# Overflow branch ahead of the slots' table, a second embedding quarter behind it, and token rows stored even columns first

## The chip, the cores and the metric

The kernel runs on one core of a Trainium2 chip. The metric is the device time of one execution in microseconds. Three runs of the kernel before gave 1337.99, 1342.89 and 1343.95, median 1342.89. Engines are named as the profile names them: PE is TensorE, PEld its weight load, DVE is VectorE, ACT is ScalarE, POOL is GpSimd, SP is SyncE.

## What is computed

Two layers of a streaming encoder over 512 tokens of 1024 columns. The first half of a layer (three kinds of attention, an output projection, a layer norm) gives the rows h. The change sits in the second half, a mixture of 16 experts, two for each token, and a gated embedding of four column quarters:

```python
scores = jax.nn.sigmoid((h @ router_w).astype(jnp.float32))
...
best_group = jnp.argmax(group_score, axis=-1)
...
_, idx = lax.top_k(masked, TOP_K)
...
for e in range(N_EXPERTS):
    hid = jax.nn.silu(h @ w_gate[e]) * (h @ w_up[e])
    out = out + gate[..., e:e + 1] * (hid @ w_down[e])
...
ple = jax.nn.sigmoid(h @ ple_gate[i]) * (p[i] @ ple_proj[i])
h = layer_norm(DEEPNORM_ALPHA * h + ffn + ple, ln2_g[i], ln2_b[i])
```

## The kernel before

Each float32 product is three matmuls of split operands (`mm3`, L213 to L215): a weight chunk of 1 MB is loaded by SP into a raw buffer, cast by ACT into a high part (L201), and DVE subtracts that to leave the low part (L203). The raw buffers are a ring that SP fills as they come free.

A layer's second half runs in these steps.

- `first_norm` makes the rows and stores them from VB to DRAM as `h1`; `rows_to_T` turns them; `logits` (L957, L958) are the router's matmuls, the last of them for token tile 0.
- The routing chain, nearly all on DVE: copy of the logits (L983, ACT), sigmoid (L984 to L987), the best group (L993 to L1008), the masked scores `msk` (L1012), the two best of each token (L1017, L1019), the one-hot tiles `oh` and their sum `mb` (L1024, L1027). PE sums `mb` into ranks (L1031 to L1035), DVE makes `rank`, and the largest count of one expert, `cmi` (L1089, L1091).
- `slot_tables`: eight one-hot tiles `ohs` (DVE, L1050) and 16 small matmuls (L1053) give `ti`, the token of each of an expert's 112 slots (L1055). `gate_parts` (L1070 to L1083) makes the gate values in three bf16 parts, `slot_gates` (L1060, L1062) moves them to the slots.
- `overflow()`: every engine loads `cmi` (L1163) and branches (L1164); the branch is taken only if an expert has over 112 tokens. Nothing of an engine's program moves across it.
- `fetch_tokens(0)` clears a buffer and gathers expert 0's rows by `ti` (POOL, L1094); `turn_tokens` (L1126) turns them by eight PE transposes of 128 columns, each a slice of every second column (`pair_columns`), since the weights of `w_gate` and `w_up` are loaded two rows to a partition.
- The loop over 16 experts: gate product g, up product u, hidden transposes (L1252), down product d, scatter with add (L1099), and the next expert's tokens. `embed(q, t)` is one quarter of the embedding for one token tile: 30 matmuls of 256 columns, a tanh (ACT, L922) and two DVE operations, the product `th` (L923) and the sum into VB (L929). Quarter 0 runs beside the routing chain; the others run within the loop, by `EMBEDS`, a table of expert to quarter.

Within each engine the order is that of a list scheduler's priorities over these calls; `after(a, [b])` adds a dependence by hand.

Of the kernel before, what the change touches and what calls it, by code (L numbers as in the profile page):

```python
# [15 lines left out]
OP = mybir.AluOpType  # L16
# [70 lines left out]
def tile_kernel(ctx, tc, A, out):  # L87
# [15 lines left out]
    TPOS = 3  # L103
# [332 lines left out]
    for l in range(L):  # L436
# [476 lines left out]
        def embed(q, t, g0, pj):  # L913

            p = acc("s" if q or t < 2 else "mm")
            for k in range(8):
                mm3(p[:, :256], hT(0, k)[:, tsl(t)], hT(1, k)[:, tsl(t)], g0[0][:, k], g0[1][:, k], k == 0, k == 7)
            for kd in range(2):
                mm3(p[:, 256:], pT[0][kd][:, tsl(t)], pT[1][kd][:, tsl(t)], pj[0][:, kd], pj[1][:, kd],
                    kd == 0, kd == 1)  # L920
            th = w2.tile([128, 512], F32, name="th", tag="w2")
            SC.activation(th[:, :256], p[:, :256], AF.Tanh, scale=0.5)  # L922
            prod = V.scalar_tensor_tensor(th[:, :256], th[:, :256], 1.0, p[:, 256:], op0=OP.add, op1=OP.mult)  # L923
            if q == 0 and t >= 2:
                after(prod, [ohs_made])
            b = base(t, 256 * q, 256 * q + 256)
            if q in scaled:
                return lambda: V.tensor_tensor(b, b, th[:, :256], op=OP.add)
            V.scalar_tensor_tensor(b, b, ALPHA, th[:, :256], op0=OP.mult, op1=OP.add)  # L929

        pows, squares = {}, {}
        LN = state["LN"]

        def first_norm(t):
# [18 lines left out]
            nc.sync.dma_start(h1_d[l][tsl(t), :], row)  # L953
# [6 lines left out]
        plg = None  # L960
        for c in MLA_REST.split():
# [3 lines left out]
            elif c[0] == "n":  # L965
                first_norm(t)
            elif c[0] == "t":
                subs, his = rows_to_T(base(t), t, tags=("tr", "av"))
            elif c[0] == "l":
# [6 lines left out]
        ew0 = gate_weights(0, (5, 7)), proj_weights(0)  # L976

# [90 lines left out]
        def gate_parts(made):  # L1068

            after(V.tensor_tensor(tmp, oh, sco[:, None].to_broadcast([128, 2, 4, 16]), op=OP.mult), [made])  # L1070
# [15 lines left out]
        ti, ohs_made, *slots = slot_tables(0, "")  # L1086
        gate_parts(ohs_made)
# [21 lines left out]
        def pair_columns(k):  # L1109
            return slice(256 * (k // 2) + k % 2, 256 * (k // 2 + 1), 2)  # L1110

        def fetch_tokens(e):
            if e == 0:
                xg = raw_chunk([], 1024)[:CAP]
            else:
# [20 lines left out]
        def expert_chunk(w, e, i):  # L1136
# [9 lines left out]
            if e == 0:  # L1146
# [14 lines left out]
        def overflow():  # L1161

            most = nc.values_load(cmi[0:1, 0:1], min_val=0, max_val=S)  # L1163
            with tc.If(most > CAP, label=f"over{l}"):  # L1164
                for j in range(1, 5):
# [7 lines left out]
                with tc.For_i(0, NE, 1) as e:  # L1173
                    for j in range(4):
# [9 lines left out]
                        for g in range(2):  # L1184
                            p = trp()
                            for jj in range(4):
                                PE.transpose(p[:, jj], xg[:, pair_columns(4 * g + jj)], ID)
# [36 lines left out]
        state["ring"].insert(TPOS, NRAW + len(FLEX))  # L1224
# [4 lines left out]
        xg = fetch_tokens(0)  # L1229
        for c in FETCHED:  # L1230
            fetched[c] = fetch_chunk(*c)
        for t in range(NT):
            embed(0, t, *ew0)
        gs = slot_gates(*slots, "")
        overflow()
        xs = turn_tokens(0, xg)
        pg = first_matmul("g", 0, xs, chunks=chunks)
        for e in range(NE):
            sg = w2.tile([128, 512], F32, name="sg", tag="w2")[:CAP]
            SC.activation(sg, pg, AF.Silu)  # L1240
# [210 lines left out]
```

## Time and profile before

| | |
|---|---|
| three runs, median | 1342.89 us |
| the profiled execution, its own time | 1344.58 us |
| its span, first to last instruction | 1342.8 us |
| TensorE busy | 1284.1 us, 96% of the span |
| VectorE busy | 1002.9 us, 75% |
| ScalarE busy | 833.8 us, 62% |
| mean granted TensorE clock | 0.976 of full |

TensorE is the engine to read: what it idles and what it runs at the lower clock is the time that can be had. Two places in each layer are touched: the handover from the router to expert 0 (about 308 to 326 us in layer 0, 968 to 987 in layer 1), and the expert loop behind it, up to about 646 and 1313.

### The profile page before, as it was taken

To read this page: it belongs to the slowest core of one execution; us is meant where nothing else is said; L and a number is where in the kernel's file an instruction comes from. 1 tells how busy PE (TensorE), PEld (TensorE's weight loads), DVE (VectorE), ACT (ScalarE), POOL (GpSimd) and SP (SyncE) were. 2 spreads that over 40 slices of the span, in tenths; PEclk is the share of its full clock that TensorE was granted. 3 is DMA by queue.
4 is the path that set the end of the run, shared out by engine and by line. 5 is a ranking of instruction groups with operands and counts; after the bars stand their busy time and mean duration, and the time that the engine had idled before them with its cause. 6 is when DMAs were issued, how large, how long until landed. Compare 5 with 4: busy or idle time off the path is not lost. (4 is left out here: it accounts for less than half of the span.)

```text
span 1342.8 us, 19139 instructions
## 1 busy us (share of the span) xinstructions
PE 1284.1 (96%) x6828; PEld 1012.9 (75%) x6828; DVE 1002.9 (75%) x1754; ACT 833.8 (62%) x1348; POOL 229.3 (17%) x209
## 2 busy tenths in 40 slices
PE   7899999998999999999889999999989999999996
PEld 6677776777787887777777777767878878778774
DVE  5645768677879879987775557676779797888985
ACT  4544645443868768886444556354467685886873
POOL 2301210001212212222001021200012121221311
PEclk9999998998999999999989999889989999999999
DMA  7732533234989979999763222341469898997983
GB/s 210 263 96 57 194 107 110 94 115 174 331 300 357 368 269 365 368 339 315 269 203 79 64 75 80 87 150 51 164 225 366 289 359 313 337 365 287 381 300 133
DMA packets 126215, 302.36 MB, mean 225 GB/s; under 512 B 13245, under 2 KB 56013, under 8 KB 126112
## 3 DMA queue, kind: packets, MB, share of 16 engines
q1 hardware_dynamic: 115400, 278.29, 57.8%
q0 software_dynamic: 9840, 21.15, 6.5%
q10 hardware_dynamic: 872, 1.62, 0.4%
q8 instruction: 55, 0.90, 0.3%
q14 instruction: 48, 0.39, 0.1%
HBM read 284.92 MB, written 30.39 MB: 235 GB/s over the span
## 5 line engine op out<-in xcount | busy, mean ns | idle before, releaser
L201 ACT CAST RA<-RAW 128x1024 fp32r<-128x1024 f32 x252 | 257.3, 1050 | 67.2 <-PE mm L215 22.9
L203 DVE TENSOR_TENSOR RA<-RAW,RA 128x1024 fp32r<-128x1024 f32 x190 | 227.5, 1222 | 59.3 <-ACT RA L201 56.3
L201 ACT CAST RA<-raw 128x1024 fp32r<-128x1024 f32 x190 | 195.7, 1048 | 61.6 <-PE mm L215 31.5
L203 DVE TENSOR_TENSOR RA<-raw,RA 128x1024 fp32r<-128x1024 f32 x142 | 168.9, 1220 | 21.2 <-ACT RA L201 20.8
L213 PE MATMUL mm<-RA,slot 128*112 128x512 f32 (+2 forms) x424 | 175.6, 415 | 4.3 <-ACT RAW L740 3.2
L215 PE MATMUL mm<-RA 128*128 128x512 f32 (+1 forms) x400 | 153.5, 384 | 0.7 <-DVE RA L193 0.7
L215 PE MATMUL mm<-RA,slot 128*112 128x512 f32 (+2 forms) x360 | 146.5, 407 | 0.0
L1099 POOL DMA_INDIRECT y<-yt,ti x30 | 64.6, 2152 | 476.0 <-ACT yt L1275 476.0
L214 PE MATMUL mm<-RA,slot 128*112 128x512 f32 (+2 forms) x344 | 141.3, 411 | 0.9 <-DVE RA L203 0.9
L213 PE MATMUL mm<-RA 128*128 128x512 f32 (+1 forms) x336 | 127.8, 381 | 5.9 <-ACT RA L201 3.7
L214 PE MATMUL mm<-RA 128*128 128x512 f32 (+1 forms) x336 | 126.7, 377 | 2.1 <-DVE RA L203 2.1
L213 PE MATMUL av<-RA 128*112 128x512 f32 x256 | 103.4, 404 | 0.8 <-ACT RA L201 0.8
L215 PE MATMUL av<-RA 128*112 128x512 f32 x256 | 101.8, 397 | 0.7 <-DVE RA L193 0.6
L213 PEld LDWEIGHTS mm<-RA,slot 128*112 128x112 f32 (+1 forms) x424 | 79.6, 188 | 26.5 <-ACT RAW L740 4.2
L213 PE MATMUL s<-RA,ht 128*112 128x512 f32 x240 | 94.9, 395 | 0.4 <-ACT ht L193 0.4
L215 PE MATMUL s<-RA,ht 128*112 128x512 f32 x240 | 94.6, 394 | 0.0
L215 PEld LDWEIGHTS mm<-RA 128*128 128x128 f32 x400 | 77.5, 194 | 12.6 <-issue 2.4
L215 PEld LDWEIGHTS mm<-RA,slot 128*112 128x112 f32 (+1 forms) x360 | 66.7, 185 | 19.7 <-issue 0.9
L214 PEld LDWEIGHTS mm<-RA,slot 128*112 128x112 f32 (+1 forms) x344 | 65.3, 190 | 18.1 <-issue 1.7
L203 DVE TENSOR_TENSOR slot<-RAW,RA 128x1024 fp32r<-128x1024 f32 x62 | 73.7, 1220 | 6.5 <-ACT RA L201 6.5
L213 PEld LDWEIGHTS mm<-RA 128*128 128x128 f32 x336 | 65.4, 195 | 15.3 <-ACT RA L201 4.1
L213 PE MATMUL s<-RA 128*128 128x256 f32 (+3 forms) x256 | 75.6, 296 | 0.5 <-ACT RA L193 0.3
(425 smaller groups left out, 2888.6 us busy)
## 6 DMA issues: line engine op xcount, KB each, us to landing
RAW<-in_w_gate_dram SPq DMA_DIRECT2D x56, 1024.0 KB
raw<-in_w_down_dram SPq DMA_DIRECT2D x45, 1024.0 KB
raw<-in_w_up_dram SPq DMA_DIRECT2D x40, 1024.0 KB
RAW<-in_w_up_dram SPq DMA_DIRECT2D x24, 1024.0 KB
RAW<-in_w_down_dram SPq DMA_DIRECT2D x19, 1024.0 KB
RAW<-in_w_in_dram SPq DMA_DIRECT2D x26, 512.0 KB
RAW<-in_w_o_dram SPq DMA_DIRECT2D x16, 512.0 KB
raw<-in_w_gate_dram SPq DMA_DIRECT2D x8, 1024.0 KB
```

The source lines that it names most:

```text
L201: cast = SC.copy(hi[:, a:b], raw[:, a:b])
L203: state["subs"] = [V.tensor_sub(lo[:, a:b], raw[:, a:b], f32(hi[:, a:b]))]
L213: PE.matmul(o, sh, mh, start=start, stop=False)
L214: PE.matmul(o, sh, ml, start=False, stop=False)
L215: return PE.matmul(o, sl, mh, start=False, stop=stop)
L1099: G.indirect_dma_start(out=dst, out_offset=bass.IndirectOffsetOnAxis(ap=idx.bitcast(U32), axis=0), in_=src, in_offset=None, bounds_check=S ...
```

## The change

In both layers:

- `overflow()` is called right behind the four `embed(0, t)`, ahead of `slot_tables`, `gate_parts`, `slot_gates` and the gather of expert 0. `gate_parts` is also repeated inside the taken branch.
- Quarter 1 of the embedding leaves the expert loop (there it ran at expert 2). Its weights are converted ahead of the branch into slots 10 and 13 (`FLEX`), and its four tiles stand behind the branch: `embed(1, 0)`, table, gate parts and gather, `embed(1, 1)`, slot gates, `embed(1, 2)`, the transposes of expert 0, `embed(1, 3)`, then the gate product. The two `FLEX` raw buffers join the ring only then. `EMBEDS` becomes `{6: 2}` in layer 0 (before `{2: 1, 6: 2}`) and `{4: 2, 9: 3}` in layer 1 (before `{2: 1, 6: 2, 10: 3}`).
- `h1` is stored from `z` after two ACT copies for each token tile (16 in all), which put the even columns of each 256 first. The transposes then read 128 columns in a row.
- The hand-written dependence of `th` of token tiles 2 and 3 on the `ohs` is gone. The casts of the first up chunks stand behind the last tanh of quarter 0, and those of expert 1's first gate chunk behind the first silu.

```diff
@@ embed @@
-            th = w2.tile([128, 512], F32, name="th", tag="w2")
-            SC.activation(th[:, :256], p[:, :256], AF.Tanh, scale=0.5)
-            prod = V.scalar_tensor_tensor(th[:, :256], th[:, :256], 1.0, p[:, 256:], op0=OP.add, op1=OP.mult)
-            if q == 0 and t >= 2:
-                after(prod, [ohs_made])
+            if t % 2 == 0:
+                state["th"] = w2.tile([128, 512], F32, name="th", tag="w2")
+            th = state["th"][:, 256 * (t % 2):256 * (t % 2) + 256]
+            tanh = SC.activation(th, p[:, :256], AF.Tanh, scale=0.5)
+            if q == 0:
+                tanhs.append(tanh)
+            V.scalar_tensor_tensor(th, th, 1.0, p[:, 256:], op0=OP.add, op1=OP.mult)
...
-            nc.sync.dma_start(h1_d[l][tsl(t), :], row)
+            return z
+
+        def store_rows(t, z, behind):
+
+            for i in range(2):
+                c = slice(512 * i, 512 * i + 512)
+                after(SC.copy(z[:, c].rearrange("p (j r i) -> p j r i", j=2, r=2),
+                              base(t)[:, c].rearrange("p (j i r) -> p j r i", j=2, r=2)), behind)
+            nc.sync.dma_start(h1_d[l][tsl(t), :], z)
...
+        ew1 = gate_weights(1, FLEX), proj_weights(1, R(9, 0, 1024, 2))
...
-        ti, ohs_made, *slots = slot_tables(0, "")
-        gate_parts(ohs_made)
...
-                    PE.transpose(p[:, jj, :CAP], xg[:, pair_columns(4 * g + jj)], ID[:CAP, :CAP])
+                    PE.transpose(p[:, jj, :CAP], xg[:, tsl(4 * g + jj)], ID[:CAP, :CAP])
...
-            elif (w, e, i) == ("u", 0, 1):
-                state["first"] = [ohs_made]
+            elif w == "u" and e == 0:
+                state["first"], state["copies"] = [ohs_made], [tanhs[-1]]
+            elif (w, e, i) == ("g", 1, 0):
+                state["copies"] = [silu]
...
-        for i, slot in enumerate(FLEX):
-            take(f"raw{NRAW + i}", F32, str(slot))
-            state["ring"].append(NRAW + i)
...
-        EMBEDS = {2: 1, 6: 2} if more else {2: 1, 6: 2, 10: 3}
+        EMBEDS = {6: 2} if more else {4: 2, 9: 3}
...
         for t in range(NT):
             embed(0, t, *ew0)
+        overflow()
+        embed(1, 0, *ew1)
+        ti, ohs_made, *slots = slot_tables(0, "")
+        gate_parts([ohs_made])
+        fetch_tokens(0, xg)
+        embed(1, 1, *ew1)
         gs = slot_gates(*slots, "")
-        overflow()
+        embed(1, 2, *ew1)
         xs = turn_tokens(0, xg)
+        embed(1, 3, *ew1)
+        for i, slot in enumerate(FLEX):
+            take(f"raw{NRAW + i}", F32, str(slot))
+            state["ring"].insert(i, NRAW + i)
```

Lines of the changed kernel stand some 1 to 14 off: 926 and 930 are `th` and VB, 1023 to 1038 the chain from `msk` to `mb`, 1042 to 1046 the rank matmuls, 1169 and 1170 the branch.

On DVE, in layer 0's routing chain, before: from the mask of the best group (`ing`) to `mb`, with nothing between.

```order
L1008 TENSOR_TENSOR ing_4212<-key_4207,fm_4210 128x64
L1012 COPY_PREDICATED msk_4214<-ing_4212,sel_4197 128x64
L1017 MAX top_4217<-msk_4214 128x8 x4
L1019 MAX_INDEX tix_4218<-top_4217,msk_4214 128x8 x4
L1021 CAST tif_4227<-tix_4218 128x8
L1011 MEMSET msk_10520 128x64
L1024 TENSOR_TENSOR oh_4229<-CT_75,tif_4227 128x128
L1027 TENSOR_TENSOR mb_4231<-oh_4229 128x64
```

The same piece of DVE's queue after (`th_4391` holds token tiles 2 and 3 of the embedding, `mm_4395` is tile 3's matmul result):

```order
L930 SCALAR_TENSOR_TENSOR VB_74<-VB_74,th_4391 128x256
L1019 TENSOR_TENSOR ing_4229<-key_4224,fm_4227 128x64
L926 SCALAR_TENSOR_TENSOR th_4391<-th_4391,mm_4395 128x256
L1023 COPY_PREDICATED msk_4231<-ing_4229,sel_4214 128x64
L930 SCALAR_TENSOR_TENSOR VB_74<-VB_74,th_4391 128x256
L1028 MAX top_4234<-msk_4231 128x8 x4
L1030 MAX_INDEX tix_4235<-top_4234,msk_4231 128x8 x4
L1032 CAST tif_4244<-tix_4235 128x8
L1022 MEMSET msk_10554 128x64
L1035 TENSOR_TENSOR oh_4246<-CT_75,tif_4244 128x128
L1038 TENSOR_TENSOR mb_4248<-oh_4246 128x64
```

The products and sums of the embedding now stand between the steps; tile 3's product stands ahead of the predicated copy that makes `msk`.

On PE, at the end of layer 0's rank matmuls (`ONB` is a matrix of ones), before: quarter 0's matmuls go on behind them.

```order
L1035 LDWEIGHTS ONB
L1035 MATMUL av<-mb,ONB 128x16
L214 MATMUL mm<-pj,RA 128x256
L215 MATMUL mm<-pj,RA 128x256
L215 MATMUL mm<-RA 128x256
```

After, the branch comes next; what follows in this listing is the taken branch's own table.

```order
L1046 LDWEIGHTS ONB
L1046 MATMUL av<-mb,ONB 128x16
L1169 TENSOR_LOAD cmi
L1170 COMPARE_AND_BRANCH
L1064 LDWEIGHTS ohs
L1064 MATMUL av<-B,ohs 128x16
```

All of quarter 0 now lies ahead of the rank matmuls, 75 of its matmuls behind the last logit, and none behind the ranks. Before, 82 lie behind the last logit: 61 ahead of the ranks, 21 behind.

On PE, at the join behind layer 0's branch, before: expert 0's transposes, then the gate product.

```order
L1164 UNCONDITIONAL_BRANCH
L1447 BRANCH_PREFETCH_HINT
L1126 MATMUL trp<-CT,RAW 128x112 x8
L213 MATMUL mm<-RA,slot_139 112x512
L214 MATMUL mm<-RA,slot_139 112x512
```

After: the first matmuls of quarter 1 (`slot_136` and `slot_137` are slots 10 and 13).

```order
L1170 UNCONDITIONAL_BRANCH
L1461 BRANCH_PREFETCH_HINT
L212 MATMUL s<-slot_136,RA 128x256
L213 MATMUL s<-slot_137,RA 128x256
L214 MATMUL s<-slot_136,RA 128x256
```

Expert 0's transposes have moved from the join to behind 90 matmuls of quarter 1.

## Rows read from the trace of the kernel before

**Rows 1.** The page, its first part: busy time, share of the span and instructions of TensorE.

```profile
PE 1284.1 (96%) x6828; PEld 1012.9 (75%) x6828; DVE 1002.9 (75%) x1754; ACT 833.8 (62%) x1348; POOL 229.3 (17%) x209
```

**Rows 2.** What TensorE waited for, whole span: us in total, times, longest us.

```profile
PE av L1060 <- DVE B L1083: 6.5, 2, 3.3
...
PE trp L1126 <- DMA RAW<-h,ti: 1.4, 1, 1.4
...
PE trp L1126 <- ACTq L1164: 1.1, 1, 1.1
```

**Rows 3.** Windows at both handovers: us; busy of PE, PEld, DVE, ACT, POOL; clock; DMA share; GB/s.

```profile
320.00:325.00 5.00, 0.85 (x11) 0.77 (x11) 5.00 (x19) 1.32 (x2) 0.99 (x1) 0.83 0.25 66
325.00:330.00 5.00, 5.00 (x16) 3.77 (x15) 1.47 (x5) 1.27 (x4) 3.73 (x4) 0.50 0.67 239
980.00:985.00 5.00, 0.77 (x10) 0.66 (x10) 5.00 (x19) 1.11 (x4) 1.09 (x1) 0.71 0.23 58
985.00:990.00 5.00, 4.99 (x19) 3.74 (x18) 1.85 (x5) 2.17 (x4) 3.04 (x4) 0.61 0.69 224
```

**Rows 4.** Timeline of layer 0's handover: start us, us, engine, line, operation; in brackets idle before.

```profile
307.71 0.26 PE L958 MATMUL av<-RW,RA 128*128 128x16 f32 x1
...
312.79 0.23 DVE L1012 COPY_PREDICATED msk<-ing,sel 128x64 f32<-128x64 uint32 x1
...
314.61 0.22 DVE L1027 TENSOR_TENSOR mb<-oh 128x64 bf16<-128x64 f32 x1
...
316.25 0.14 DVE L1091 CAST cmi<-cmx 128x1 int32<-128x1 f32 x1
...
319.20 0.28 PE L215 MATMUL mm<-pj,RA 128*128 128x256 f32 x1
...
319.88 1.12 POOL L1094 DMA_INDIRECT RAW<-h,ti  x1 [20.90 <-DVE den L1075]
...
322.77 0.36 PE L1060 MATMUL av<-B,ohs 128*128 128x48 bf16 x8 [3.29 <-DVE B L1083]
...
326.12 0.77 PE L213 MATMUL mm<-RA,slot 128*112 128x512 f32 x1
```

**Rows 5.** Timeline of TensorE at layer 1's handover, the same columns.

```profile
968.20 0.26 PE L958 MATMUL av<-RW,RA 128*128 128x16 f32 x1
...
986.46 0.77 PE L213 MATMUL mm<-RA,slot 128*112 128x512 f32 x1
```

**Rows 6.** The branch's instructions by source line: duration ns min/median/max, first and last start.

```profile
L1163 PEldq TENSOR_LOAD <-cmi x2: 310/311/312, 322.8 to 983.2; - x2
...
L1164 PEldq COMPARE_BRANCH  x2: 331/338/344, 323.2 to 983.6; - x2
```

**Rows 7.** Timeline of VectorE, two operations that the changed order puts into the routing chain.

```profile
307.49 1.22 DVE L203 TENSOR_TENSOR slot<-RAW,RA 128x1024 fp32r<-128x1024 f32 x1
...
322.09 0.42 DVE L929 SCALAR_TENSOR_TENSOR VB<-VB,th 128x256 f32<-128x256 f32 x1
```

**Rows 8.** A window of embedding matmuls alone, columns as in rows 3.

```profile
308.02:313.27 5.25, 5.25 (x46) 5.25 (x45) 4.87 (x19) 0.82 (x3) 0.00 (x0) 1.00 0.40 115
```

**Rows 9.** The token and hidden transposes: weight loads by source line, then the timeline in expert 8.

```profile
L1126 PEld LDWEIGHTS trp<-CT,xg x240: 194/215/221, 333.8 to 1294.3; 112*128 112x128 f32 x120
...
L1252 PEld LDWEIGHTS trp<-CT,sg x128: 137/140/143, 343.6 to 1315.3; 112*128 112x128 f32 x128
...
511.48 1.10 PE L1126 MATMUL trp<-CT,xg 112*128 112x112 f32 x8
...
517.29 0.55 PE L1252 MATMUL trp<-CT,sg 112*128 112x112 f32 x4
```

**Rows 10.** Expert stage, experts 7 to 12: a window, ScalarE's wait, then the gathers' DMA.

```profile
500.00:520.00 20.00, 20.00 (x95) 15.34 (x94) 18.14 (x19) 17.15 (x21) 4.80 (x3) 1.00 1.00 354
...
ACT RA L201 <- DMA raw<-in_w_up_dram: 3.0, 2, 2.3
...
DMA to landing us min/median/max: 4.3/8.9/10.8
```

More of the change, by code (lines that the diff above doesn't have):

```diff
@@ L920, in embed @@
                     kd == 0, kd == 1)
[L921 to L925 removed]
+            if t % 2 == 0:
[5 more added lines that the diff above has]
+            V.scalar_tensor_tensor(th, th, 1.0, p[:, 256:], op0=OP.add, op1=OP.mult)
             b = base(t, 256 * q, 256 * q + 256)
             if q in scaled:
[L928 to L931 removed]
+                return lambda: V.tensor_tensor(b, b, th, op=OP.add)
+            V.scalar_tensor_tensor(b, b, ALPHA, th, op0=OP.mult, op1=OP.add)
+        pows, squares, tanhs = {}, {}, []
         LN = state["LN"]
@@ L958, in logits @@
                 PE.matmul(plg[:, t, :16], hT(1, k)[:, tsl(t)], RW[:, k, :16], start=False, stop=k == 7)
-        plg = None
+        plg, normed = None, {}
         for c in MLA_REST.split():
@@ L965, in tile_kernel @@
             elif c[0] == "n":
-                first_norm(t)
+                normed[t] = first_norm(t)
             elif c[0] == "t":
                 subs, his = rows_to_T(base(t), t, tags=("tr", "av"))
+                store_rows(t, normed[t], his)
             elif c[0] == "l":
@@ L1068, in gate_parts @@
         def gate_parts(made):
-            after(V.tensor_tensor(tmp, oh, sco[:, None].to_broadcast([128, 2, 4, 16]), op=OP.mult), [made])
+            after(V.tensor_tensor(tmp, oh, sco[:, None].to_broadcast([128, 2, 4, 16]), op=OP.mult), made)
             gate = sm.tile([128, 2, 4], F32, name="gate", bufs=1)
@@ L1105, in tile_kernel, with fetch_tokens @@
         wdn = A["w_down"][l].rearrange("e (k p) c -> e p k c", p=128)
[L1109 to L1115, printed above, removed]
+        def fetch_tokens(e, xg=None):
+            if xg is None:
                 xg = w4.tile([128, 1024], F32, name="xg", tag="w4")[:CAP]
@@ L1164, in overflow @@
             with tc.If(most > CAP, label=f"over{l}"):
+                gate_parts([])
                 for j in range(1, 5):
@@ L1186, in overflow @@
                             for jj in range(4):
-                                PE.transpose(p[:, jj], xg[:, pair_columns(4 * g + jj)], ID)
+                                PE.transpose(p[:, jj], xg[:, tsl(4 * g + jj)], ID)
                             SC.copy(xt[:, 4 * g:4 * g + 4], p)
@@ L1219, in tile_kernel @@
         take("slot15", F32R)
-        for i, slot in enumerate(FLEX):
-            take(f"raw{NRAW + i}", F32, str(slot))
-            state["ring"].append(NRAW + i)
         take(f"raw{NRAW + len(FLEX)}", F32, str(TEMP))
-        state["ring"].insert(TPOS, NRAW + len(FLEX))
+        state["ring"].append(NRAW + len(FLEX))
         BETWEEN = 3
         more = l + 1 < L
-        EMBEDS = {2: 1, 6: 2} if more else {2: 1, 6: 2, 10: 3}
+        EMBEDS = {6: 2} if more else {4: 2, 9: 3}
         chunks = [expert_chunk("g", 0, i) for i in range(2)]
-        xg = fetch_tokens(0)
+        xg = raw_chunk([], 1024)[:CAP]
         for c in FETCHED:
@@ L1239, in tile_kernel @@
             sg = w2.tile([128, 512], F32, name="sg", tag="w2")[:CAP]
-            SC.activation(sg, pg, AF.Silu)
+            silu = SC.activation(sg, pg, AF.Silu)
             xn = turn_tokens(e + 1, fetch_tokens(e + 1)) if e + 1 < NE else None
```

3 lines of the change are left out of this document (1 added, 2 removed).

## The prediction

> **What bounds the kernel now.** I read the page's first part first. TensorE is busy 96% of the span [rows 1], so only its idle time, its time at the lower clock and the length of its own instructions can be had. Then its waits: of those in the region of the change, the slot gates wait 3.3 us in each layer for the gate values (6.5 in all), and expert 0's transposes 1.4 us for the gathered rows in one layer and 1.1 us for the branch in the other [rows 2]. Then the windows: TensorE does 0.8 us of work in 320 to 325 and 980 to 985, the granted clock is 0.83 and 0.71 there, and 0.50 (the 1.2 GHz level) through 325 to 330, 0.61 in 985 to 990 [rows 3]. So an idle of about 5 us is followed by several us at half speed. The timeline shows the chain behind it: last logit, routing on DVE, ranks, `cmi`, end of the embedding, gates, branch, transposes, gate product [rows 4, 5].
>
> From the end of the last logit (307.97; 968.46) to the first gate matmul (326.12; 986.46) are 18.15 and 18.0 us [rows 4, 5]. Behind that point the clock is still at half speed, in layer 0 to about 330.0 and in layer 1 to 985 + 5 x (1 - 0.61) / 0.5 = 988.9 [rows 3], which loses another half of 3.9 and of 2.4 us: 1.9 and 1.2. Quarter 1 ran at expert 2, beside nothing that it covers: 120 matmuls. A stretch of embedding matmuls alone has 46 in 5.25 us with two cut by its edges [rows 8], 0.118 each, so 14.2. What the change must beat, from the last logit to the gate product with quarter 1 done, at full clock: **34.25 in layer 0, 33.4 in layer 1**.
>
> **The change part by part.** *The routing chain.* DVE works in order, so each operation put into the chain delays `cmi`. Before, the chain is bare; `cmi` ends at 316.39 [rows 4], 8.4 behind the last logit, hidden by 82 embedding matmuls. After, the eight products and sums of quarter 0 stand within it, and tile 3's product stands ahead of the predicated copy. That product waits for the last of the 75 matmuls behind the last logit: 75 x 0.118 = 8.9, 9.05 with the first one's start. Then a tanh and a product, each about 0.4 (the sum has 0.42 [rows 7]): copy at about 9.9. Low and high parts of the first gate chunk (1.22 each on DVE [rows 7]) also stand among the sigmoid's steps, but end by then. From the copy's start to the end of `mb` are 2.04 (312.79 to 314.83), with one sum of 0.33 more: 12.25. From `mb` to `cmi`'s end 1.56 (314.83 to 316.39) [rows 4]: 13.8. Load and branch on TensorE's queue, 0.31 and 0.34 [rows 6]: 14.5, first matmul at **14.6**. TensorE is idle from 9.05 to 14.6 but for 0.5 of rank matmuls: about 5.0 us, where it had 3.3 + 1.4 before. I conclude that the wait is moved from the gates to the branch and not removed; every engine stops at the branch, so quarter 1 can't fill it.
>
> *Behind the branch.* Quarter 1's 14.2, the table's matmuls 1.3 (before, 307.97 to 319.48 is 11.5, of which 82 x 0.118 = 9.7 are embedding and 0.5 ranks), the slot gates 0.4 (0.36 [rows 4]), transposes 0.8. Now the gates' chain on DVE has quarter 1 to hide behind, as it should: about 3 us of small operations beside 5.2 us of matmuls. If that cover failed it would cost the 3.3 of before. The gather starts once `ti` is there, with 44 matmuls and the gates left ahead of the transposes, 5.6 us. Before, it was issued at 319.88 [rows 4], five embedding matmuls and 0.4 behind the table, so 1.0; landing takes 4.3 at least and 8.9 at the median [rows 10]: a wait of 0 to 4.3. I take 1.3, near the low end, because the 4.3 is nearest: few loads are on the way behind the branch, as at the gathers of before there (DMA share 0.25 [rows 3]). The clock falls as before, since TensorE is idle as long; before, from the transposes on, half speed lasted some 5.5 us in layer 0 and 4.2 in layer 1, so 2.1 to 2.75 are lost; I take 2.2.
>
> 14.6 + 14.2 + 1.3 + 0.4 + 0.8 + 1.3 + 2.2 = 34.8. The last logit itself comes later by seven embedding matmuls that now stand ahead of it (0.8), and by a layer norm step that queues behind the new conversions of quarter 1's weights on DVE, at most one of 1.22 [rows 7], taken as 0.4: 36.0. So the handover is **slower by 1.75 in layer 0 and 2.6 in layer 1, 4.35 in all**; with the bounds of the gather (-1.3 to +3.0 each), the clock (-0.1 to +0.5) and the norm (-0.4 to +0.8), between 0.7 and 13.
>
> *The rows' order.* The token transposes load every second column: 215 ns a weight load, where the hidden transposes, from neighbouring columns, take 140 [rows 9]. A group of eight takes 1.10 us and a group of four 0.55; less about 0.26 for the last one's own length that is 0.120 and 0.097 for one: 0.18 saved in a group of eight. There are 30 groups in the expert loops (15 a layer), where TensorE has no other wait in 500 to 520 (20.00 of 20 busy, 95 instructions [rows 10]): **-5.4**. From below it is bounded by nothing saved, from above by 30 x 0.23 = 7 (whole groups' shares, 0.109 against 0.08 for one). The 16 copies for it, 512 columns each, are on ACT beside the norms; tile 0's two stand in its queue ahead of the logits' copy, in place of a cast. The nearest row is 1.22 for 1024 columns on DVE [rows 7], so about 0.6 each. I cost them at nothing; if ACT comes late with the logits' copy, at most two of them show, 1.2 a layer, and then only as far as tile 3's product doesn't set the chain anyway.
>
> The Trainium skill, "Advanced Engine Details and Errata", section "SBUF Cachelines", speaks against this part: SBUF is read in 16-byte lines and two hits on a line are enough for full speed. Every second float32 hits each line twice, so by that rule the old slices were already at full speed and the 5.4 would be 0. The loads of 215 against 140 ns [rows 9] disagree, and I go by the rows.
>
> *The weight stream.* An expert is 84 TensorE instructions, 17.7 us at 95 in 20 us, and needs 6.29 MB of weights and 0.46 of tokens: 381 GB/s. Delivered are 354 at a DMA share of 1.00 [rows 10], so each expert draws some 0.48 MB from what is buffered, and embedding quarters refill it. Nine experts in a row, 7 to 15 in layer 0, were carried before; casts begin to wait for a load (2.3 us at most [rows 10]), TensorE does not. After, the longest new stretch is seven, experts 0 to 6 of layer 0. I cost it at nothing; the third rival prices it.
>
> **Sum.** +4.35 - 5.4 = -1.05 on the profiled execution's 1344.58: 1343.5. That execution lies 1.69 above the median of 1342.89, so **1341.9**.
>
> **The rivals.**
>
> *Faster: the branch comes early enough.* If the scheduler's order doesn't bind as I read it (the embedding's sums done in DVE's gaps, `cmi` only the eight of them late: 8.4 + 8 x 0.33 = 11.0, restart at 11.8), the idle is 2.8 less, and the shorter idle costs less clock, about 1 us less: 3.8 a layer, 1341.9 - 7.6 = 1334.3. With `cmi` at 8.4 as before and no loss of clock it would be 7 a layer: 1328. For it: 9.05 us of matmuls cover the bare chain's 8.4. Against it: tile 3's product stands ahead of the copy.
>
> *Slower: the stream runs dry in layer 0.* At the gate product only four raw buffers can be ahead, where six were in the ring, and the refill at expert 2 is gone. Seven experts draw 7 x 0.48 = 3.4 MB. If that isn't buffered when the loop starts, TensorE waits for casts from about expert 4 on: 3.4 MB at 354 GB/s is 9.5 us, and the transposes' gain of those experts (7 x 0.18 = 1.3) goes with it: 1341.9 + 10.8 = 1352.7. It decides from a reserve of under 3.4 MB; for it speak the casts' waits of 2.3 us in the sixth expert behind an embedding, against it the nine experts without a wait of TensorE.
>
> *Nothing saved in the transposes.* If the eight transposes are set by something other than the load of their columns (the group of four also differs in its results' length), the 5.4 are 0: 1347.3. This is the time that the page's rule gives. For it: a matmul's 0.120 is shorter than its load of 0.215, so loads overlap; against it: 0.120 and 0.097 are the pace itself.
>
> **How the numbers follow.** Forecast 0.45 (own range 1336 to 1349, from the bounds of the gather and the transposes), the faster rival 0.27, the slower 0.16, no saving 0.12. Likeliest: 1341.9. The range reaches to part of both outer rivals: 1332 to 1351. About 0.5% is what a measurement of this kernel can tell from no change, 6.7 us: faster means under 1336.2, slower over 1349.6. Faster 0.28, the same 0.55, slower 0.17.
>
> **What would show it.** Right: on TensorE, an idle of 4 to 6 us with the rank matmuls in it, released by the branch's load, about 9 us behind the last logit, then half clock on quarter 1's first matmuls; the waits for the gate values gone; the first gate matmul 35 to 37 us behind where the last logit was before; token weight loads near 140 ns and groups of eight near 0.92 us; no embedding at expert 2. Wrong: an idle of under 2 us there or a clock that stays at 1.00 (the faster rival); waits for casts in experts 3 to 6 of layer 0 (the slower one); loads of 140 ns with the pace unchanged (the last).

## The result, and the profile after

The changed kernel is **slower**: 1352.33 us median of five runs (1350.52 to 1356.31) against 1341.0 of five of the kernel before (1337.99 to 1343.95). The ratio is 1.009, 95% interval 1.0074 to 1.0106. The forecast was 1341.9, no change.

The profiled execution after took 1351.29 us, its span is 1349.5. That of before, 1344.58, lies 3.6 above the median of its five runs. The execution after lies 1.0 below its own. So the two traces differ by 6.7 us where the medians differ by 11.3, and the traces can place only those 6.7.

The page's first part, after (busy us, share of the span, instructions), beside [rows 1]:

```profile
PE 1280.6 (95%) x6828; PEld 1009.3 (75%) x6828; DVE 1003.8 (74%) x1754; ACT 842.7 (62%) x1364; POOL 212.0 (16%) x209
```

TensorE is busy 3.5 us less than before in a span that is 6.7 longer: it waits more. Its waits (us in total, times, longest us), for [rows 2]:

```profile
PE av L1042 <- DVE mb L1038: 6.2, 2, 3.1
...
PE s L212 <- DVEq L1170: 3.9, 2, 2.0
...
PE av L1071 <- DVE B L1094: 2.2, 2, 1.1
...
PE trp L1130 <- issue: 2.1, 1, 2.1
...
PE trp L1130 <- DMA RAW<-h,ti: 1.7, 1, 1.7
PE av L1064 <- DVE ohs L1061: 1.6, 2, 0.8
```

DVEq is VectorE's sequencer, which runs the branch (L1170). The wait for the gate values (6.5 before) is 2.2. In its place stand 6.2 for `mb` ahead of the branch, 3.9 at the branch, 1.6 for the one-hot tiles and 3.8 for expert 0's gathered rows (one of these two is put down to "issue"): 17.7 us where before had 9.0. The windows (us; busy of PE, PEld, DVE, ACT, POOL; granted clock; DMA share; GB/s), for [rows 3]:

```profile
320.00:325.00 5.00, 3.37 (x16) 3.40 (x17) 0.97 (x7) 0.00 (x0) 1.84 (x2) 0.50 0.04 8
325.00:330.00 5.00, 4.21 (x37) 3.89 (x36) 1.03 (x5) 1.67 (x2) 0.00 (x0) 0.95 0.00 0
335.00:340.00 5.00, 1.90 (x21) 1.59 (x19) 3.52 (x9) 0.58 (x2) 2.58 (x3) 0.92 0.82 291
340.00:345.00 5.00, 4.90 (x24) 4.93 (x25) 1.25 (x2) 1.06 (x2) 0.00 (x0) 0.50 0.53 168
345.00:350.00 5.00, 5.00 (x29) 4.32 (x28) 1.02 (x3) 1.44 (x2) 0.00 (x0) 0.90 0.65 229
380.00:385.00 5.00, 5.00 (x19) 3.65 (x18) 4.04 (x5) 2.41 (x4) 0.00 (x0) 0.66 1.00 374
985.00:990.00 5.00, 3.68 (x17) 3.71 (x18) 0.73 (x5) 0.00 (x0) 1.59 (x2) 0.50 0.05 10
1005.00:1010.00 5.00, 5.00 (x32) 5.00 (x32) 1.25 (x2) 1.06 (x2) 0.00 (x0) 0.68 0.59 187
```

The clock is at 0.50 twice in layer 0's handover: in 320 to 325, behind the branch, and again in 340 to 345, behind a second idle (1.90 of 5 us busy in 335 to 340). Before it fell once there. Layer 1 has the same two (0.50 in 985 to 990, 0.68 in 1005 to 1010). A third fall, 0.66 in 380 to 385, lies in the step from expert 0 to expert 1 of layer 0; it comes up again with the loop's start. The timeline of layer 0 shows each step (start us, us, operation; in brackets the idle ahead of it), for [rows 4]:

```profile
306.75 0.26 PE L967 MATMUL av<-RW,RA 128*128 128x16 f32 x1
...
315.77 0.28 PE L214 MATMUL mm<-pj,RA 128*128 128x256 f32 x1
319.14 0.22 PE L1042 MATMUL av<-mb,TRB 128*128 128x16 bf16 x2 [3.09 <-DVE mb L1038]
...
321.63 0.55 PE L212 MATMUL s<-slot,RA 128*128 128x256 f32 x1 [1.95 <-DVEq L1170]
...
329.61 0.21 PE L1064 MATMUL av<-B,ohs 128*128 128x16 bf16 x2 [0.79 <-DVE ohs L1061]
...
337.45 0.36 PE L1071 MATMUL av<-B,ohs 128*128 128x48 bf16 x8 [1.11 <-DVE B L1094]
...
340.10 1.73 PE L1130 MATMUL trp<-CT,RAW 112*128 112x112 f32 x8 [2.09 <-issue]
...
347.15 0.39 PE L212 MATMUL mm<-RA,slot 128*112 128x512 f32 x1
```

From the end of the last logit (307.01): quarter 0 ends at 9.0, the first rank matmul starts at 12.1, the first matmul behind the branch at 14.6, the gate product at 40.1. VectorE and GpSimd in the same stretch:

```profile
316.51 0.42 DVE L926 SCALAR_TENSOR_TENSOR th<-th,mm 128x256 f32<-128x256 f32 x1 [0.39 <-ACT th L923]
...
318.86 0.22 DVE L1038 TENSOR_TENSOR mb<-oh 128x64 bf16<-128x64 f32 x1
...
328.97 0.42 DVE L926 SCALAR_TENSOR_TENSOR th<-th,s 128x256 f32<-128x256 f32 x1 [6.64 <-ACT th L923]
...
330.66 1.22 DVE L202 TENSOR_TENSOR RA<-raw,RA 128x1024 fp32r<-128x1024 f32 x1
...
334.33 0.17 DVE L1091 CAST gb<-gate 128x8 bf16<-128x8 f32 x1
...
334.84 1.75 DVE L1091 CAST gb<-gate 128x8 bf16<-128x8 f32 x1
...
334.59 1.00 POOL L1103 DMA_INDIRECT xg<-h,ti  x1 [0.30 <-issue]
335.58 0.97 POOL L1121 MEMSET xg<- 112x1024 f32 x1
```

The first two rows are the end of the routing chain: tile 3's product waited for its tanh (316.51), and `mb` ends at 319.08. At 328.97 the product of quarter 1's first tile stands between two one-hot tiles and holds the rest back: VectorE has been idle for 6.64 us until its tanh was there. Two low parts of the first up chunks, 1.2 us each (the first at 330.66), then stand ahead of the gate values. At 334.84 a cast of 128 by 8 takes 1.75 us, where its twin takes 0.17, while GpSimd issues a gather and clears the next tile (334.59 to 336.55). TensorE gets the gate values only at 337.45.

The token transposes themselves, for [rows 9]. The start of each expert's hidden transposes marks its place in the loop, and the step from one to the next is the loop's pace; two of them, experts 3 and 4, are shown:

```profile
L1130 PEld LDWEIGHTS trp<-CT,xg x240: 137/140/146, 352.5 to 1302.3; 112*128 112x128 f32 x120
...
419.20 0.55 PE L1266 MATMUL trp<-CT,sg 112*128 112x112 f32 x4
...
437.03 0.55 PE L1266 MATMUL trp<-CT,sg 112*128 112x112 f32 x4
```

A weight load is 140 ns where it was 215, and an expert takes 17.83 us where it took 18.01 to 18.03.

### The profile page after: what moved, and what is told of

The parts are those of the page before. It is cut to its first block, busy times and chain, and to the rows that moved or that the text cites. A ratio compares the mean times of both kernels' runs of the same rounds, so it can differ in the third digit from the quotient of the medians.

```text
span 1349.5 us, 19098 instructions
## 1 busy us (share of the span) xinstructions
PE 1280.6 (95%) x6828; PEld 1009.3 (75%) x6828; DVE 1003.8 (74%) x1754; ACT 842.7 (62%) x1364; POOL 212.0 (16%) x209
## 5 line engine op out<-in xcount | busy, mean ns | idle before, releaser
L200 ACT CAST RA<-RAW 128x1024 fp32r<-128x1024 f32 x254 | 261.1, 1050 | 74.8 <-PE mm L214 27.1
L202 DVE TENSOR_TENSOR RA<-RAW,RA 128x1024 fp32r<-128x1024 f32 x154 | 185.4, 1222 | 58.0 <-ACT RA L200 54.8
L202 DVE TENSOR_TENSOR RA<-raw,RA 128x1024 fp32r<-128x1024 f32 x178 | 212.1, 1220 | 21.9 <-ACT RA L200 21.2
L200 ACT CAST RA<-raw 128x1024 fp32r<-128x1024 f32 x184 | 187.8, 1050 | 24.6 <-PE av L214 8.5
L212 PE MATMUL mm<-RA,slot 128*112 128x512 f32 (+2 forms) x424 | 173.6, 410 | 5.0 <-ACT RAW L739 3.3
L213 PE MATMUL mm<-RA,slot 128*112 128x512 f32 (+1 forms) x372 | 150.4, 405 | 0.9 <-DVE RA L202 0.9
L214 PE MATMUL mm<-RA,slot 128*112 128x512 f32 (+2 forms) x360 | 145.9, 405 | 1.0 <-DVE slot L192 1.0
L202 DVE TENSOR_TENSOR slot<-RAW,RA 128x1024 fp32r<-128x1024 f32 x100 | 119.7, 1219 | 19.3 <-ACT RA L200 19.3
L1108 POOL DMA_INDIRECT y<-yt,ti x30 | 52.4, 1745 | 485.0 <-ACT yt L1289 485.0
L212 PE MATMUL av<-RA 128*112 128x512 f32 x256 | 103.0, 402 | 1.0 <-ACT RA L200 0.7
L214 PE MATMUL av<-RA 128*112 128x512 f32 x256 | 101.2, 396 | 0.2 <-DVE RA L192 0.2
L213 PEld LDWEIGHTS mm<-RA,slot 128*112 128x112 f32 (+1 forms) x372 | 68.9, 185 | 19.6 <-DVE RA L202 1.9
L213 PE MATMUL av<-RA 128*112 128x512 f32 x204 | 80.1, 393 | 0.4 <-DVE RA L202 0.4
L212 PEld LDWEIGHTS mm<-RA 128*128 128x128 f32 x336 | 65.1, 194 | 14.6 <-ACT RA L200 3.6
```

Source lines behind the costliest of these rows:

```text
L200: cast = SC.copy(hi[:, a:b], raw[:, a:b])
L202: state["subs"] = [V.tensor_sub(lo[:, a:b], raw[:, a:b], f32(hi[:, a:b]))]
L212: PE.matmul(o, sh, mh, start=start, stop=False)
L213: PE.matmul(o, sh, ml, start=False, stop=False)
L214: return PE.matmul(o, sl, mh, start=False, stop=stop)
L1108: G.indirect_dma_start(out=dst, out_offset=bass.IndirectOffsetOnAxis(ap=idx.bitcast(U32), axis=0), in_=src, in_offset=None, bounds_check=S ...
```

## The experiments

Each run's ratio is to the runs of the kernel before on the same chip (1340.9, 1342.2 and 1340.6 us for the three sets). The changed kernel stands at 1.009. Differences in us are between medians, some of them taken on different chips; by the ratios e5 stands 12.7 us and e10 20 us below the changed kernel, where the medians give 10.6 and 16.6. Diffs are against the changed kernel unless said, and are excerpts. The text calls a run by its first part (e7 is e7_branch_late).

| kernel | median us | ratio, 95% interval |
|---|---|---|
| e1_strided | 1351.4 | 1.0075, 1.0059 to 1.0091 |
| e2_rows_only | 1350.4 | 1.0065, 1.0043 to 1.0086 |
| e4_products | 1350.4 | 1.0076, 1.0059 to 1.0094 |
| e12_branch_only | 1355.2 | 1.0096, 1.008 to 1.0113 |
| e5_turn_last | 1341.7 | 0.9995, 0.9983 to 1.0007 |
| e10_no_branch | 1335.7 | 0.994, 0.9916 to 0.9964 |
| e7_branch_late | 1333.8 | 0.9953, 0.9938 to 0.9969 |
| e8_late_strided | 1335.4 | 0.9942, 0.9924 to 0.996 |
| e7_again | 1333.1 | 0.995, 0.9931 to 0.997 |
| e8_again | 1335.8 | 0.9962, 0.9943 to 0.9981 |
| e13_fetch_more | 1330.0 | 0.9926, 0.9897 to 0.9955 |
| e14_copy_pool | 1336.7 | 0.9972, 0.9947 to 0.9996 |

### The rows' order, undone and alone

```diff
-                    PE.transpose(p[:, jj, :CAP], xg[:, tsl(4 * g + jj)], ID[:CAP, :CAP])
+                    PE.transpose(p[:, jj, :CAP], xg[:, pair_columns(4 * g + jj)], ID[:CAP, :CAP])
...
-                store_rows(t, normed[t], his)
+            nc.sync.dma_start(h1_d[l][tsl(t), :], row)
```

> The changed kernel with its rows stored from VB in their own order and every second column taken in the transposes, as before; all else as changed. Theory (the rows' order saves about 5 us in the expert loops, the moved branch loses about 11 in the two handovers): the token groups of eight go back from 0.93 to 1.09 us and an expert from 17.83 to 18.0, so 5 to 6 us slower than the changed kernel, about 1357.5. Rival (the 16 copies on ScalarE or the later stores cost what the transposes save): within 2 us of the changed kernel's 1352.3.

Measured: 1351.4, as fast as the changed kernel with its contiguous slices (intervals of the ratios overlap). The theory's number fell, the rival's held. Hidden transposes of experts 3 and 4 in this run:

```profile
417.72 0.55 PE L1269 MATMUL trp<-CT,sg 112*128 112x112 f32 x4
...
435.69 0.55 PE L1269 MATMUL trp<-CT,sg 112*128 112x112 f32 x4
```

The pace is 17.97, so the transposes do save 0.14 to 0.18 an expert, and yet the sum doesn't show it. Ahead of the ranks TensorE waits 2.2 and 2.3 us for `mb` in this run, where it is 3.1 after the change: some of what the order saves in the loop is lost there. Whether the copies or the scheduler's new order does that isn't shown.

The same part alone, on the kernel before (the diff is that of the change, lines on `store_rows` and `tsl`):

> The kernel before with the rows' order alone (copies, stores from z, contiguous transposes); branch, gates and quarter 1 where they were. Theory: 4 to 6 us faster than the kernel before, about 1336. Rival (the loop gives the saving back to the weight stream, which delivers 354 GB/s at a DMA share of 1.00): within 2 us of before.

Measured: 1350.4, **slower** than before by 9.5. Both theories fell here. In its trace the wait for the gates, and VectorE's queue around the one-hot tiles, read:

```profile
PE av L1069 <- DVE B L1092: 8.2, 2, 4.1
...
315.87 1.23 DVE L203 TENSOR_TENSOR RA<-raw,RA 128x1024 fp32r<-128x1024 f32 x1
...
318.89 1.22 DVE L1059 TENSOR_SCALAR ohs<-IOB,rank 128x128 bf16<-128x128 bf16 x7
```

With the copies in ScalarE's queue the scheduler puts low parts of the first up chunk (the first at 315.87) ahead of the one-hot tiles (318.89), which TensorE waits for (before, they stand behind the gate values, at 322.63); the wait for the gates is 4.1 us in each layer, 0.8 more than before. The clock loses more as well: it is at 0.75 in 330 to 335 and at 0.88 in 990 to 995, where before had 0.99 and 1.00, and it falls once more in layer 1's loop (0.78 in 1030 to 1035). So this run tells of that order too, and not of the stride alone. Its trace is 5.6 us longer than that of before, so the rest of the 9.5 isn't placed. The changed kernel holds those casts back by hand.

### The products in the routing chain

```diff
-            V.scalar_tensor_tensor(th, th, 1.0, p[:, 256:], op0=OP.add, op1=OP.mult)
+            prod = V.scalar_tensor_tensor(th, th, 1.0, p[:, 256:], op0=OP.add, op1=OP.mult)
+            if q == 0:
+                after(prod, [counted])
```

> The changed kernel with quarter 0's four products (and with them its sums) behind the count that the branch reads, so that the routing chain on VectorE is bare again but for the four low-part subtractions. Theory (those products make TensorE idle ahead of the branch): the sum of the one-hot tiles ends some 2.7 us earlier, the idle around the rank matmuls falls from 5.0 to about 2.3 us in each layer, 5 to 8 us faster than the changed kernel, about 1346, more if the clock then doesn't fall. Rival (the loss lies behind the branch, in the second idle and the clock's second fall): under 2 us faster, since the wait only moves to behind the branch.

Measured: 1350.4, 2 us less than the changed kernel, with intervals that overlap, and not 5 to 8: the rival's side. The wait for `mb` is nearly gone, and another has grown:

```profile
PE s L212 <- DVEq L1172: 7.9, 2, 4.0
```

It was 3.9 in all after the change. The products now stand between the count and VectorE's own branch, and quarter 1's first matmul waits for that. The first idle moves along with them: this order on VectorE doesn't cure it, and no other was tried.

### The branch ahead, alone

Against the kernel before: the branch ahead of table, gates and gather, quarter 1 still at expert 2, rows strided.

```diff
+        overflow()
+        ti, ohs_made, *slots = slot_tables(0, "")
+        gate_parts([ohs_made])
+        fetch_tokens(0, xg)
         gs = slot_gates(*slots, "")
-        overflow()
```

> The kernel before with the branch ahead of table, gates and first gather, and nothing else changed but that quarter 0's last two products no longer wait for the one-hot tiles; quarter 1 stays at expert 2, rows strided. Theory (the branch ahead costs an idle of 5 us at the branch that quarter 1 can't fill, and without quarter 1 the table, gather and gates stand bare behind it): the first gate matmul comes some 25 us behind the last logit where it came 18 before, 6 to 8 us a layer, about 1355. Rival (the branch ahead is harmless, and it is quarter 1 that costs): within 5 us of the kernel before, under 1346.

Measured: 1355.2, 13 us more than before, as the theory had it; the gate product comes 24.4 and 25.1 us behind the last logit. The branch ahead is the part that costs: table, gates and gather stand bare behind it, each with its wait on TensorE, and the clock is at 0.50 in 325 to 330:

```profile
321.96 1.09 PE L1051 MATMUL av<-B,ohs 128*128 128x16 bf16 x16 [4.04 <-DVE ohs L1048]
325.62 0.48 PE L1058 MATMUL av<-B,ohs 128*128 128x48 bf16 x8 [2.57 <-DVE B L1081]
330.05 1.74 PE L1120 MATMUL trp<-CT,RAW 112*128 112x112 f32 x8 [3.95 <-issue]
...
325.00:330.00 5.00, 0.48 (x8) 0.34 (x7) 0.88 (x5) 1.48 (x2) 3.23 (x4) 0.50 0.69 234
```

### The second idle

```diff
         embed(1, 1, *ew1)
-        gs = slot_gates(*slots, "")
         embed(1, 2, *ew1)
-        xs = turn_tokens(0, xg)
         embed(1, 3, *ew1)
+        gs = slot_gates(*slots, "")
+        xs = turn_tokens(0, xg)
```

> The changed kernel with the slots' gates and expert 0's transposes behind all four tiles of quarter 1 instead of behind the second and third; the branch stays ahead. Theory (the second idle, 1.1 us for the gates and 2.1 for the gathered rows, and the half clock that follows it cost about 5 us a layer): both waits fall under 0.5 us, the clock stays up behind the transposes, about 1 us of waiting for their split operands comes new: 3 to 4 us a layer less, about 1345. Rival (the first idle at the branch is all that counts): within 2 us of the changed kernel's 1352.3.

Measured: 1341.7, ratio 0.9995: 10.6 us less than the changed kernel, more than was expected. Layer 0's first matmul behind the branch, its gate product, and a window:

```profile
322.74 0.55 PE L212 MATMUL s<-slot,RA 128*128 128x256 f32 x1 [1.95 <-DVEq L1170]
...
342.80 0.48 PE L212 MATMUL mm<-RA,slot 128*112 128x512 f32 x1 [0.24 <-ACT slot L192]
...
340.00:345.00 5.00, 4.76 (x39) 4.01 (x39) 2.03 (x6) 1.52 (x5) 0.00 (x0) 1.00 0.86 308
```

The idle at the branch is as it was (1.95). The waits for gates and gather are gone, 6.0 us for both layers together, and the clock stays at 1.00 in 340 to 345. The windows of the changed kernel give the price of the second half-speed stretch: from 340.1 to 346.0 in layer 0 (0.90 in 345 to 350 is 1.0 us at half), half of it lost, 2.95; from 1004.8 to 1008.2 in layer 1 (0.68 is 3.2 us at half), 1.7. 6.0 + 4.65 less 0.5 for the new waits (0.24 in layer 0) is 10.2 of the 10.6. In the traces the way from last logit to gate product is 34.65 and 34.62 us, 5.5 and 4.4 shorter than in the changed kernel.

### No branch, and the branch late

Without the branch (it leaves out the second pass for experts with over 112 tokens):

> The changed kernel without the overflow branch, all else in the same order of calls; it leaves out the second pass for experts with over 112 tokens. Theory (the branch's place is what costs, since no instruction passes it): TensorE goes from quarter 0 straight to quarter 1, no idle over 2 us and no half clock in either handover, 18 to 22 us faster than the changed kernel, 1330 to 1334, near the kernel with the branch behind quarter 1 (1333.8). Rival (quarter 1's operations in VectorE's queue delay the table and the gather whatever the branch does): waits for the one-hot tiles and for the gathered rows stay, 1340 or more.

Measured: 1335.7, 16.6 less than the changed kernel. The idle at the ranks is gone. In layer 0 the gather still comes late behind 60 matmuls, and the clock falls once:

```profile
PE trp L1130 <- DMA RAW<-h,ti: 2.0, 1, 2.0
...
330.00:335.00 5.00, 2.98 (x15) 2.98 (x16) 2.45 (x6) 1.48 (x4) 0.00 (x0) 0.64 0.47 133
```

So the theory's number nearly held, and its sentence on the clock did not: the wait for the rows belongs to the place of the transposes, as in the run before. Of the rival, waits for gates and rows stay (in layer 1 1.2 and 1.1 us, with the clock at 1.00), but its time of 1340 or more fell.

With the branch kept, but behind all of quarter 1 and the gates, where only the transposes are left to wait for it:

```diff
-        overflow()
         embed(1, 0, *ew1)
...
         embed(1, 2, *ew1)
-        xs = turn_tokens(0, xg)
         embed(1, 3, *ew1)
...
+        overflow()
+        xs = turn_tokens(0, xg)
```

> The changed kernel with the branch behind all four tiles of quarter 1 and the slots' gates, ahead of the transposes only, as the kernel before had it; the repeated gate values in the taken branch are left out, since they are made ahead of it here. Theory (what costs is that nothing of quarter 1 can pass the branch, so that TensorE idles twice and the clock falls twice): 202 embedding matmuls cover routing, table, gates and gather, TensorE idles only 1 to 3 us at the branch, 8 to 9 us a layer less than the changed kernel: about 1336, below the kernel before. Rival (the embedding ahead of the expert loop costs in itself, by a weight stream that starts with fewer buffers): the loop's first experts wait for casts, and the time stays above 1345.

Measured: 1333.8 and, run again, 1333.1: faster than the kernel before by 0.5%. Layer 0's handover:

```profile
330.97 0.37 PE L1071 MATMUL av<-B,ohs 128*128 128x48 bf16 x8
...
335.41 0.98 PE L1130 MATMUL trp<-CT,RAW 112*128 112x112 f32 x8 [0.67 <-ACTq L1170]
337.38 0.48 PE L212 MATMUL mm<-RA,slot 128*112 128x512 f32 x1 [0.98 <-ACT slot L192]
...
335.00:340.00 5.00, 3.61 (x19) 2.79 (x20) 2.00 (x4) 2.85 (x5) 2.82 (x3) 1.00 0.64 220
```

The gates have no wait, the branch 0.67, the split operands of the transposes 0.98, and the clock stays at 1.00. From the last logit (309.12) to the gate product are 28.3 us, against 40.1 after the change and 34.25 before with quarter 1 counted in. This kernel differs from the changed one in two things, the branch's place and that of gates and transposes, and is 18.5 us faster. The second alone gave 10.6 (e5), the branch taken out alone 16.6 (e10). The two overlap and can't be added.

### The rows' order again, and the loop's start

> The kernel with the branch behind quarter 1, its rows stored in their own order from VB and every second column taken in the transposes. It is the kernel before with quarter 1 ahead of the expert loop as its main difference. Theory (contiguous transposes shorten an expert by 0.17 us, and where the loop's start doesn't stall this shows): 3 to 5 us slower than 1333.8, about 1338. Rival (what they save is waited for at the loop's start or in the stream): within 1.5 us of 1333.8.

Measured: 1335.4. The ratios of the two, 0.9942 here and 0.9953 with the rows' new order, have intervals that overlap. Side by side on one chip:

> The kernel with the branch behind quarter 1, unchanged, beside its strided twin on the same chip. Theory (the loop's starts stall by the program's order, not by chance): again about 1334, with a stall of 2 us in layer 0's first expert and of 4 us between experts 1 and 2 of layer 1. Rival (chance): other experts stall, or none.

> The strided twin of the kernel with the branch behind quarter 1, on the same chip. Theory (the rows' order shortens each expert by 0.17 us and costs about as much in copies on ScalarE and in stalls at the loop's start): within 2 us of the twin. Rival (the first pair of runs hid a saving of 5 us by the chip's spread): 4 us or more slower than the twin.

Measured: 1333.1 and 1335.8, 2.7 us apart with intervals that overlap (0.9931 to 0.997, 0.9943 to 0.9981). Between the two expectations. By the ratios the two are 0.0012 apart, 1.6 us, and a saving of 5 lies at the edge of what the intervals leave. The stalls at the loop's starts recurred at the same places (19.9 and 19.6 us for expert 0 to 1 in layer 0, 22.06 and 22.13 for expert 1 to 2 in layer 1, where the pace is 17.83): program order, not chance. Part of each is again the clock. In e7_again TensorE waits 0.92 and 1.03 us for split operands, at 1037.66 and 1039.40, and then runs at a lower clock:

```profile
1040.00:1045.00 5.00, 5.00 (x19) 3.68 (x18) 3.88 (x4) 2.47 (x3) 0.00 (x0) 0.67 1.01 362
```

These waits and half of the low stretch (0.67 of 5 us is 3.3 us at half) are 3.6 of the 4.3 us. Without the branch (e10) the same steps take 17.83 and 17.84 us in both layers: no stall. A wait of ScalarE in layer 0, ahead of the first weighted output, from the changed kernel's timeline, isn't explained by that:

```profile
367.27 2.00 ACT L200 CAST RA<-RAW 128x1024 fp32r<-128x1024 f32 x2 [0.56 <-PE s L214]
372.30 0.69 ACT L1289 ACTIVATE yt<-s,gs 112x512 f32<-112x512 f32 x1 [3.02 <-PE av L214]
```

The wait is 3.4 us in e7_again. What ends it isn't settled: TensorE had long been done, and the trace puts one packet of an instruction queue (q14) between 370 and 371, ahead of the restart at 372.3, and one at the same distance ahead of the restart in e7_branch_late. That ScalarE waited for code was not tried.

```diff
             state["ring"].insert(i, NRAW + i)
+        fetched["d", 0, 1] = fetch_chunk("d", 0, 1)
         overflow()
```

> The kernel with the branch behind quarter 1 and the second half of expert 0's down weights asked for ahead of the branch, in the first of the two raw buffers that quarter 1 leaves. Theory (the first experts stall because the loads start late): the stalls of 2 and 4 us at the loop's starts go, 3 to 5 us faster, about 1330. Rival (what stalls is ScalarE's queue, not a load): within 1.5 us of its twin.

Measured: 1330.0, 3 less than its twin of the same set, as the theory had it: **0.7% faster than the kernel before, 1.6% faster than the changed one**. The intervals of the twins overlap (0.9897 to 0.9955, 0.9931 to 0.997), so it is the trace that decides. Hidden transposes of experts 1 and 2 in layer 1, e7_again:

```profile
1021.25 0.55 PE L1265 MATMUL trp<-CT,sg 112*128 112x112 f32 x4
...
1043.38 0.55 PE L1265 MATMUL trp<-CT,sg 112*128 112x112 f32 x4
```

and e13_fetch_more:

```profile
1018.57 0.55 PE L1266 MATMUL trp<-CT,sg 112*128 112x112 f32 x4
...
1036.40 0.55 PE L1266 MATMUL trp<-CT,sg 112*128 112x112 f32 x4
```

22.1 us have become 17.83, at a clock of 1.00. A load that starts ahead of the branch does away with that stall. The first interval of layer 0 is still 18.8, against 19.6.

```diff
-                after(SC.copy(z[:, c].rearrange("p (j r i) -> p j r i", j=2, r=2),
+                after(G.tensor_copy(z[:, c].rearrange("p (j r i) -> p j r i", j=2, r=2),
```

> The kernel with the branch behind quarter 1 and its 16 row copies on GpSimd instead of ScalarE. Theory (the copies' place in ScalarE's queue, ahead of casts and of the logits' copy, costs some 1.2 us a layer between the last logit and expert 0): 2 us faster than its twin, about 1332. Rival (GpSimd's copies are slower, and the gather or the norm's steps wait for it): 2 us or more slower.

Measured: 1336.7, 3.6 more than its twin, with intervals that overlap; the rival's side. Layer 0's handover is as long as the twin's (42.9 and 43.0 us from the last logit to expert 0's hidden transposes). The loop's first step is longer (21.7 against 19.6 in layer 0, 20.3 against 18.6 in layer 1), layer 1's second one shorter (17.9 against 22.1). The theory's gain of 1.2 a layer between last logit and expert 0 isn't there. The two traces are only 1.0 us apart, so the rest of the 3.6 isn't placed, and whether the copies cost as much on GpSimd as on ScalarE isn't separated.

### Where the time lies, by stretch

From the starts of the hidden transposes in each trace, with 14.2 us of expert 2's embedding moved ahead of the loop for the kernel before (e7 and e8 are e7_branch_late and e8_late_strided):

| stretch | before | changed | e1 | e7 | e8 |
|---|---|---|---|---|---|
| start to expert 0, layer 0 | 358.0 | 361.8 | 362.4 | 352.2 | 351.9 |
| expert 0 to 15, layer 0 | 287.2 | 285.5 | 285.0 | 285.0 | 285.7 |
| to expert 0, layer 1 | 371.5 | 378.1 | 376.5 | 365.6 | 369.4 |
| expert 0 to 15, layer 1 | 298.3 | 296.2 | 298.8 | 301.5 | 298.8 |

The contiguous slices (changed and e7) should save 15 x 0.17 = 2.6 in each loop against the strided (e1 and e8). They show 2.6 only in layer 1 of the first pair. In layer 0 the changed kernel lost it in one interval (expert 0 to 1, 21.7 against 19.4 in e1), e7 in layer 1 in another (22.06). In the interval of 21.7 the changed kernel waits 0.78 and 1.03 us for split operands and the clock falls to 0.66 in 380 to 385; e1 idles 0.8 us in all and stays at 1.00. So the saving went into a second short wait and the fall of the clock behind it.

## Why the prediction was wrong

**The chain to the branch: right.** `mb` was to end at 12.25 us behind the last logit and the first matmul behind the branch to come at 14.6. They came at 12.07 and 14.6. The idle of 5.0 was 3.09 + 1.95. That the wait is moved and not removed, and that the clock falls behind it, held: 1.9 us lost there in layer 0 and 2.4 in layer 1, 2.2 forecast. The profile of before showed this idle [rows 2, 3], and the order showed where it would go.

**Behind the branch: wrong by 5.3 and 4.2 us.** The step said that the gates' chain has quarter 1 to hide behind, "as it should", that the gather waits 1.3, and that the clock falls once. 34.8 us were forecast from last logit to gate product; 40.1 and 39.0 were measured. The failing terms:

- The waits: 0.79 for the one-hot tiles, 1.11 for the gates, 2.09 for the rows, 4.0 in layer 0 and 3.6 in layer 1, forecast 1.3. I counted VectorE's small operations as 3 us beside 5.2 of matmuls, and not what stood in its queue ahead of them: quarter 1's own products (6.64 us of idle ahead of the first one, for a tanh behind a table load of 1.28), two low parts of 1.2 each, and a cast that took 1.75 beside GpSimd. The gather landed in 7.2 us; I had taken 4.3 as the nearest row, with 8.9 as the bound, because of a DMA share of 0.25, and it was 0.82 in 335 to 340.
- The clock's second fall, 2.95 and 1.7, was not in the sum. I had the first idle's price from the rows of before, and did not ask what a second idle of 3 us behind it would do. The run with the transposes last shows both together: 10.6 us. That an earlier idle is needed for this fall isn't so: in e10 waits of 0.68 and 2.02 us, with no fall before them, brought it too.

With the restart, quarter 1, table, slot gates and transposes as forecast, the three waits and the two losses of the clock: 14.6 + 14.2 + 1.3 + 0.4 + 0.8 + 4.0 + 1.9 + 2.95 = 40.15 for layer 0, of 40.1 measured. With 3.6, 2.4 and 1.7 for layer 1 it is 39.0, of 39.0. No further term is needed.

**The rows' order: the pace right, the gain wrong.** The forecast of 140 ns a load, 0.92 us a group and 0.18 an expert held (137 to 146 ns, 0.93, 0.17). The 5.4 us did not come: the loops of the changed kernel are 3.8 shorter than before, those of e1, strided, 1.7; undone, the kernel was as fast (e1), and beside the late branch the order was worth 2.7 by the medians of one pair, 1.6 by its ratios, with intervals that overlap; in the other pair the strided kernel had the lower ratio. Where it went is shown in part: in the step from expert 0 to 1 of layer 0 (21.7 us, with two waits and a fall of the clock), not in the steady loop. I had called the loop free of other waits from one window in its middle [rows 10]; its starts are not. The Trainium skill, "Advanced Engine Details and Errata", section "SBUF Cachelines", would have given 0 for this part. In the time of the whole kernel the part came out near that, but not for that reason, since the loads did get shorter by a third.

**The account.** In the traces the handovers grew by 40.1 - 34.25 and 39.0 - 33.4, 11.45; the last logit of layer 0 came 1.0 earlier, and the expert loops are 3.8 shorter: 6.65 of the 6.7 us between them. Two pieces left out of this cancel: from gate product to expert 0's hidden transposes it is 1.2 shorter in the two layers together (at full clock), and from layer 0's last expert to layer 1's last logit 1.2 longer. So the last logit's delay, forecast as 1.2 in each layer, came in layer 1 only. Forecast were +4.35 for the handovers with the last logit's delay, and -5.4 for the loops: 6.1 and 1.6 off. The last 2.7 of the miss of 10.4 is the step from execution to median: I took 1.7 off, where the changed kernel's execution was 1.0 below its median.

**The rivals.** The slower one (1352.7) gave the right time by luck: the stream did not run dry in experts 3 to 6, which ran at 17.83 to 17.85 with no wait for casts. The mechanism that decided, stalls behind the branch with a second fall of the clock, was in no rival; its pieces stood in the bounds of the gather (up to 4.3) and of the gates (3.3), each taken at its cheap end. The handovers' bounds, 0.7 to 13, did hold the measured 10.45. At their dear end the sum is 1350.5, and 1355.9 without the transposes' saving; the stated range of 1332 to 1351 was narrower than its own terms.

## What to carry to other kernels

Work that is to fill a wait has to be able to run in it: a barrier that every engine stops at belongs behind the filler, not ahead of it. Here the branch behind the filler, with gates and transposes behind the filler too, was worth 18.5 us; with the branch left ahead, moving gates and transposes alone was worth 10.6. Where an idle precedes a fall of the clock, each idle is priced with the half-speed stretch behind it, and a step that is "covered" by time is covered only if its engine's queue has nothing else ahead. A shorter instruction in a steady loop is a gain only if the loop's start, with its own waits and the clock behind them, doesn't take it back: undo the part alone and measure.

## What the runs showed of the hardware

- A DVE cast of 128 by 8 took 1.35 to 1.78 us instead of 0.17 where it stood beside GpSimd's gather issue and clearing of 112 by 1024 (both layers of the changed kernel, e1, e4, e5 and e10), ending with the clearing (336.59 against 336.55). Beside a gather's issue alone it took 0.16 (at 336.91, the issue from 336.82 to 337.85), and it took 0.17 where the gathers came at another time (e7: 163 to 172 ns in all six).
- In layer 0 TensorE stood for 1.11 and 2.09 us with a few matmuls between, and the granted clock was 0.50 in 340 to 345, though it had been 0.95 and 0.92 since the first fall. With idles of 0.67 and 0.98 in the same place (e7) it stayed at 1.00. In e10, without an earlier fall, idles of 0.68 and 2.02 us were followed by 0.64 in 330 to 335, and idles of 1.2 and 1.1 in layer 1 by 1.00.
